# Padding the small SBUF tiles so that every large tile starts at the same byte modulo 128, in a two-layer hybrid decoder trunk

## The chip, the cores and the metric

The kernel runs on one core of a Trainium2 chip. Its engines are named as the profile names them: PE is TensorE (matrix products), PEld its weight loads, DVE is VectorE, ACT is ScalarE, POOL is GpSimd, and SP is SyncE, which issues most of the DMA transfers. The metric is the device time of one execution in microseconds (us), taken as the median of several runs. Of one execution there is a profile with the start and length of every instruction.

SBUF is the memory on the core that the engines read their operands from: 128 partitions, each a row of bytes. A tile occupies the same byte range in all partitions, so a tile has one start address. In this text "the place of a tile" is that start address modulo 128 bytes.

## What is computed

A stream of 1024 positions by 1024 channels in float32 goes through two layers, each followed by a gated MLP, with an RMS norm ahead of each part and a residual add behind it.

```python
def reference(x, ...):
    h = x
    for layer in range(DEPTH):            # DEPTH = 2
        if layer % 2 == 0:
            h = h + even_mixer(rmsnorm(h, mix0_norm), ...)
        else:
            h = h + odd_mixer(rmsnorm(h, mix1_norm), ...)
        h = h + conv_glu_ffn(rmsnorm(h, ffn_norm[layer]), ...)
    return rmsnorm(h, final_norm)

def even_mixer(x, ...):
    xa, ga, c_pre, b_post, vb = jnp.split(x @ w_in, [W, 2 * W, 2 * W + C, 2 * W + 2 * C], axis=-1)
    xa = causal_depthwise_conv(xa, lru_conv_w, lru_conv_b)
    ya = rg_lru(xa, lru_wa, lru_ba, lru_wx, lru_bx, lru_lambda) * jax.nn.gelu(ga)
    yb = b_post * causal_depthwise_conv(c_pre * vb, sconv_w, sconv_b)
    return jnp.concatenate([ya, yb], axis=-1) @ w_out

def odd_mixer(x, ...):
    z, q, k, v, f = jnp.split(x @ w_in, [Z, Z + F, Z + 2 * F, Z + 3 * F], axis=-1)
    u, g = jnp.split(jax.nn.gelu(z), 2, axis=-1)
    yc = chunked_spatial_gating(u, g, sgu_norm, sgu_w, sgu_b)   # 128-position chunks
    yd = forgetting_attention(q, k, v, f, fox_bf)               # 8 heads of 64, 128-query blocks
    return jnp.concatenate([yc, yd], axis=-1) @ w_out

def conv_glu_ffn(x, w_up, conv_w, conv_b, w_down):              # 1024 -> 2 x 2816 -> 1024
    gate, val = jnp.split(causal_depthwise_conv(x @ w_up, conv_w, conv_b), 2, axis=-1)
    return (jax.nn.silu(gate) * val) @ w_down
```

`rg_lru` makes two sigmoid gates by block-diagonal products (64x64 blocks), and runs a gated linear recurrence over the positions.

## The kernel before

Everything is kept transposed, channels on the partitions and positions along the row. Each float32 operand of a product is split into a high part (rounded to the format that PE reads in one pass) and a low part, the remainder; a product is three matmuls, high by high, high by low, low by high, each 128x128 weights by 512 positions. The normalized stream stands in `AH` (high) and `AL` (low) for the whole run. Weights come by DMA into `wst`, ACT casts the high part into `wh`, and DVE subtracts to get the low part `wl`.

The stages follow each other in program order, with each engine's instructions in the order in which the code writes them:

- **mix0** (line 1275 on): projections; for each of four channel groups the convolution `xc`, its split `xh` and `xl`, the gate products `ra` and `ix` (line 1347), and the elementwise tiles `gg`, `r`, `ig`, `w`, all from the pool `l0` that opens with the small tile `lsm` of 40 numbers.
- **out_proj0** and **blocks**: output projections into the residual tiles `hT` (`hT_o` in the traces), which `open_h` (line 308) puts at the far end of SBUF in two halves of four channel groups, each with a pool of its own. DVE adds each product to `hT` (line 557), a copy goes to DRAM, ACT squares it, and `Norm.chunk` (line 355) normalizes it into `AH` and `AL`; for four of the eight channel groups of a half POOL makes the low part.
- **ffn**: a loop over 22 groups of hidden channels with products by a seven-product scheme on blocks (line 676), results `X` and `YZ` in PSUM, DVE and ACT work on `g`, `v`, `cg`, `cv`; hidden values go to DRAM. Then eight "quads" of down-projection products (line 942) that add into `hT` (`hT_f`), and plain products (line 1152) that add the rest (line 1154). All loads of weights and hidden values are issued by SP.
- **mix1**: q, k, v and spatial-gating projections (line 1452) woven with attention. For each head, `S` is the product of `qs` with `kh` and `kl` (lines 1583 and 1584), DVE combines it with the decay row `cb` (line 1597), ACT exponentiates, PE transposes the result and multiplies it by `vv` (line 1617). The tiles of heads 3 and 7 (`qs`, `kh`, `kl`, `vv`) and `cb` of odd heads come from the pool `keep`, those of all other heads from the pool `rest`, together with the spatial-gating tiles `gain`, `wth`, `wtl`, `gsm`, `gvh`, `gvl`. The weave is a fixed list of numbers of steps and knows nothing of addresses.

Where a tile lies follows from the sizes of the tiles allocated ahead of it. The pool `const` comes first: `eps`, `junk`, `ident`, `ones`, `AH`, `AL`, the parameter columns `par_a` (96 numbers a partition), and four tiles `par_c` of the MLPs' convolution taps (88 numbers each, made in `load_rows`, line 269). Behind them come the weight buffers, the temporaries, and the stage's own pools. `hT` is allocated from the other end.

Of the kernel before, what the change touches and what calls it, by code (L numbers as in the profile page):

```python
# [8 lines left out]
F32 = mybir.dt.float32  # L9
# [7 lines left out]
P = 128  # L17
T = 1024
H = 512
D = 1024  # L20
DC = 8
NH = 8
HD = 64
DFF = 2816
NF = DFF // P
# [43 lines left out]
def weave(main, fill, pace, done=0, stop=None):  # L69


    for pos in main:
        want = pace(pos)
        while done < want and fill is not None:
            if next(fill, "end") == "end":
                fill = None
            done += 1
        if stop is not None and pos >= stop:
            break
    if fill is not None:  # L80
        run(fill)
# [75 lines left out]
def trunk(ctx: ExitStack, tc: tile.TileContext, x, mix0_norm, mix0_w_in, lru_conv_w, lru_conv_b,  # L157
# [4 lines left out]
    pe, act, dve, pool = nc.tensor, nc.scalar, nc.vector, nc.gpsimd  # L162
# [63 lines left out]
    cp = ctx.enter_context(tc.tile_pool(name="const", bufs=1))  # L226
# [8 lines left out]
    def t2(name):  # L235
        return tmp.tile([P, H], F32, tag="t2", bufs=4, name=name)
# [19 lines left out]
    def psml(name):  # L256
        return sml.tile([P, H], F32, tag="sml", name=name)
# [11 lines left out]
    def load_rows(name, groups):  # L269

        n = sum(r for _, r in groups)
        raw = t2(f"raw_{name}")[:, :P]
        at, offs = 0, []
        for ap, r in groups:
            nc.sync.dma_start(raw[at:at + r, :], ap)
            offs.append(at)
            at += r
        t = cp.tile([P, n], F32, name=f"par_{name}")
        return t, offs, raw, n

    def turn_rows(t, offs, raw, n):
        ps = psml("pt")
        pe.transpose(ps[:, :n], raw[:n, :], ident[:n, :n])
        dve.tensor_copy(t, ps[:, :n])
        return t

    def r1(ap):
# [20 lines left out]
    def open_h(name):  # L308
        st["pool"], tiles = [], []
        for i in (1, 0):  # L310
            cm = tc.tile_pool(name=f"h{i}_{name}", bufs=1, side="right")
            st["pool"].append(cm)
            tiles.insert(0, cm.__enter__().tile([P, 4, T], F32, name=f"hT{i}_{name}"))
        st["hT"] = Halves(tiles)

    def close_h():
# [102 lines left out]
    class Start:  # L419
# [68 lines left out]
        def second(self, beside):  # L488


            steps = {"q": self.squares, "r": self.root, "s": self.scale, "h": self.high,
                     "l": self.low}

            def do(ops, *behind):
                for op in ops.split():
                    with ExitStack() as after:
                        for ins in behind:
                            after.enter_context(tc.issue_after(ins.ins))
                        steps[op[0]](int(op[1]))

            behind = last["act"], last["dve"]
            do("q4 r4 q5 r5 s4 h4 l4 q6 r6 s5 h5 l5 q7 r7 s6 s7", *behind)
            do("h6 l6 h7 l7", beside(*behind))
            turn_rows(*par_rows)
            sp_cm.__exit__(None, None, None)

    norm = [Start()]
    for tt in range(4):
# [3 lines left out]
        if tt == 0:  # L512
            nc.sync.dma_start(g0, mix0_norm.partition_broadcast(P))
    W._dma()
    par_rows = load_rows("a", [
        (r1(mix0_norm), 8), (lru_conv_w[0].rearrange("k (c p) -> (k c) p", p=P), 16),
        (r1(lru_conv_b), 4), (r1(lru_ba), 4), (r1(lru_bx), 4), (r1(lru_lambda), 4),
# [12 lines left out]
    class Out:  # L530


        def __init__(self, ly):
            self.ly = ly
            open_h(f"o{ly}")
            self.hT = st["hT"]
            if ly:
                for s in HALF:
                    for c in range(DC):
                        nc.sync.dma_start(self.hT[:, c, s], hdr[:, c, s])  # L540
            g = gcols[order[order.index(f"mix{ly}") + 1]]
            self.norms = [Norm(h, g, f"no{ly}", put=True) for h in range(2)]
# [49 lines left out]
    def load_cw(ly):  # L592

        w = [ffn_conv_w[ly, k].rearrange("(c p) -> c p", p=P) for k in range(3)]
        b = ffn_conv_b[ly].rearrange("(c p) -> c p", p=P)
        rows = (load_rows(f"c{ly}0", [(w[0], 44), (w[1], 44)]),
                load_rows(f"c{ly}1", [(w[2], 44), (b, 44)]))

        def turn():
            cw[ly] = [turn_rows(*r) for r in rows]  # L600

        return turn
# [6 lines left out]
    def ffn(ly, norms):  # L609
# [469 lines left out]
        for cm in reversed(w2_cm):  # L1079
            cm.__exit__(None, None, None)  # L1080
        fd_cm.__exit__(None, None, None)
        open_h(f"f{ly}")
        hT = st["hT"]

# [190 lines left out]
    def mix0(norms):  # L1275
# [19 lines left out]
        Y = ypl.tile([P, DC, T], F32, name="Y0")  # L1295
        lp = tc.tile_pool(name="l0", bufs=1)
        pl = lp.__enter__()
        small = pl.tile([P, 40], F32, name="lsm")


        lam = par[:, o_lam:o_lam + 4]
# [114 lines left out]
    def mix1(norms):  # L1416
# [6 lines left out]
        keep, rest = keep_cm.__enter__(), rest_cm.__enter__()  # L1423
        lo, hi = slice(0, HD), slice(HD, P)

# [37 lines left out]

        fraw = rest.tile([P, DC, NH], F32, name="fraw")
        pool.dma_start(fraw, mix1_w_in[0, :, 2560:2568].rearrange("(k p) m -> p k m", p=P))
# [5 lines left out]
        dve.tensor_tensor(sel, ident[0:16, 0:8], ident[0:16, 8:16], op=ALU.add)  # L1471
        cdr = dram.tile([NH, T], F32, name="cdr")
        ydr = dram.tile([P, DC, T], F32, name="ydr")
# [30 lines left out]
        def load_c(h_):  # L1504
            cbs[h_] = (keep if h_ % 2 else rest).tile([P, T], F32, tag="cb", name=f"cb{h_}")
            nc.sync.dma_start(cbs[h_], cdr[h_:h_ + 1, :].partition_broadcast(P))

        def qkv(pr, first=False):
# [3 lines left out]
            def stack(tag, h_, shape):  # L1512
                if (tag, h_) not in stk:
                    p_, n_ = (keep, 1) if h_ % 4 == 3 else (rest, 3 if tag == "qs" else 2)
                    stk[tag, h_] = p_.tile(shape, F32R, tag=tag, bufs=n_, name=f"{tag}{h_}")
                return stk[tag, h_]

            def tail_q(ps, s, hh):
                for h_, r, nr in sides:
                    q = stack("qs", h_, [P, T])  # L1520
                    act.activation(q[r, s], ps[r], AF.Copy, scale=-(HD ** -0.5))
                    dve.scalar_tensor_tensor(q[nr, s], ps[r], -(HD ** -0.5),
                                             q[r, s].bitcast(F32), op0=ALU.mult, op1=ALU.subtract)
# [45 lines left out]
        def attn(h_):  # L1569
            qs, kh = stk["qs", h_], stk["kh", h_]  # L1570
            r0 = HD * (h_ % 2)
            rows = slice(r0, r0 + HD)
            kl, cb = stk["kl", h_], cbs[h_]
# [32 lines left out]
            def pv(g):  # L1606
# [38 lines left out]
                act.copy(yt[lo], acc[0][hi, :256])  # L1645
                if h_ == NH - 1:
                    at = rows, 7, slice(256 * g, 256 * g + 256)
# [9 lines left out]
        def chain(heads):  # L1657


            prev = None  # L1660
            for h_ in heads:
                soft, pv = attn(h_)
                n = 0
                for step in steps(soft, pv, prev, h_):
                    n += 1
                    yield h_ + min(n / 22, 0.999)
                prev = pv
            for _ in prev(3):
                n += 1
                yield h_ + min(n / 22, 0.999)  # L1670

        def steps(soft, pv, prev, h_):
# [3 lines left out]
            soft(1)  # L1676
            if h_ + 1 < NH:
                load_c(h_ + 1)
# [8 lines left out]
                yield from pv(g)  # L1687


        mhalf = rest.tile([P, 8], F32, name="mhalf")  # L1690
        pool.memset(mhalf, -0.5)

        def sgu(c):
# [22 lines left out]
            def norm_g(gz, s, hh):  # L1716
# [7 lines left out]
                v, r, q = sm[:, 0], sm[:, 1], sm[:, 2]  # L1724
                dve.tensor_reduce(v, sq.rearrange("p (n d) -> p n d", d=HD), axis=AX.X, op=ALU.add)
                dve.tensor_scalar(v, v, 1.0 / HD, EPS, op0=ALU.mult, op1=ALU.add)
# [58 lines left out]
        for _ in range(LEAD):  # L1785
            next(filler)
        heads = chain(range(NH))
        weave(heads, filler,
# [52 lines left out]
        for oc in range(DC):  # L1841
            ps = o_.block(1, oc)
# [5 lines left out]
    for s_ in order[:-1]:  # L1848
        if s_ == "mix0":
            norm = mix0(norm)  # L1850
        elif s_ == "mix1":
            norm = mix1(norm)
        else:
            norm = ffn(int(s_[-1]), norm)
# [35 lines left out]
```

## Time and profile before

| | |
|---|---|
| three runs | 2132.11, 2132.75 and 2134.26 us, median 2132.75 |
| the profiled execution | 2131.98 us, of which the profile's span is 2130.3 us |
| PE busy | 2093.4 us, 98% of the span |
| DVE busy | 1599.0 us, 75% |
| ACT busy | 1068.4 us, 50% |
| POOL busy | 75.4 us, 4% |
| DMA queues | 249.98 MB, the main one 36.5% of 16 engines |

The span runs from the first to the last instruction of the profiled execution; the 1.7 us beside it are start and end of the launch. Busy times of engines overlap, so they don't add up to the span. A group of instructions in the profile has its line, engine, operation, output and inputs, the number of instructions, their busy time in all, and the mean length of one in ns; behind it stands the idle time ahead of the group and what ended it. A busy PE is modelled: matmuls are pipelined, so a matmul of 512 columns is shown with some 390 ns although the next one starts earlier.

### The profile page before, as it was taken

To read this page: it belongs to the slowest core of one execution; us is meant where nothing else is said; L and a number is where in the kernel's file an instruction comes from. 1 tells how busy PE (TensorE), PEld (TensorE's weight loads), DVE (VectorE), ACT (ScalarE), POOL (GpSimd) and SP (SyncE) were. 2 spreads that over 40 slices of the span, in tenths; PEclk is the share of its full clock that TensorE was granted. 3 is DMA by queue.
4 is the path that set the end of the run, shared out by engine and by line. 5 is a ranking of instruction groups with operands and counts; after the bars stand their busy time and mean duration, and the time that the engine had idled before them with its cause. 6 is when DMAs were issued, how large, how long until landed. Compare 5 with 4: busy or idle time off the path is not lost. (4 is left out here: it accounts for less than half of the span.)

```text
span 2130.3 us, 25849 instructions
## 1 busy us (share of the span) xinstructions
PE 2093.4 (98%) x9673; PEld 1719.2 (81%) x9673; DVE 1599.0 (75%) x2290; ACT 1068.4 (50%) x1493; POOL 75.4 (4%) x121
## 2 busy tenths in 40 slices
PE   8999999999999999999999999999999999999998
PEld 7888888788888888888778888788788888878887
DVE  6655647998888777875566766868998888777875
ACT  5333534654555555333556575744655455555323
POOL 0000001000000000000111111101000000000000
PEclk9999999999999999999999999999999999999999
DMA  4111342333323267752221212442333233267732
GB/s 150 56 50 41 108 154 94 95 113 109 104 96 107 80 206 253 242 173 74 75 58 54 75 56 59 156 153 89 104 104 119 94 116 97 80 228 248 240 104 80
DMA packets 269318, 249.98 MB, mean 117 GB/s; under 512 B 10224, under 2 KB 222000, under 8 KB 269192
## 3 DMA queue, kind: packets, MB, share of 16 engines
q1 hardware_dynamic: 268856, 247.83, 36.5%
q8 instruction: 76, 1.25, 0.2%
q0 software_dynamic: 192, 0.30, 0.1%
q14 instruction: 50, 0.41, 0.1%
q10 hardware_dynamic: 144, 0.20, 0.0%
HBM read 181.93 MB, written 64.26 MB: 116 GB/s over the span
## 5 line engine op out<-in xcount | busy, mean ns | idle before, releaser
L129 ACT CAST wh<-wst 128x1024 fp32r<-128x1024 f32 (+1 forms) x87 | 86.3, 992 | 223.4 <-PE op L376 45.2
L129 DVE TENSOR_TENSOR wl<-wst,wh 128x1024 fp32r<-128x1024 f32 (+1 forms) x87 | 100.0, 1150 | 96.6 <-ACT wh L129 96.5
L676 PE MATMUL X<-TH,wh 128*128 128x512 f32 x384 | 150.0, 391 | 1.8 <-ACT u L1034 1.4
L676 PE MATMUL X<-TH,wl 128*128 128x512 f32 x384 | 149.7, 390 | 0.7 <-DVE wl L370 0.7
L676 PE MATMUL X<-TL,wh 128*128 128x512 f32 x384 | 149.4, 389 | 0.0
L369 ACT CAST wh<-wst 128x1024 fp32r<-128x1024 f32 x96 | 100.3, 1051 | 74.6 <-PE YZ L676 49.5
L370 DVE TENSOR_TENSOR wl<-wst,wh 128x1024 fp32r<-128x1024 f32 x96 | 116.5, 1218 | 11.9 <-ACT wh L369 11.9
L698 DVE SCALAR_TENSOR_TENSOR cg<-g,par_c,cg 128x1023 f32<-128x1023 f32 x88 | 112.8, 1281 | 7.3 <-ACT cg L692 6.1
L698 DVE SCALAR_TENSOR_TENSOR cv<-v,par_c,cv 128x1023 f32<-128x1023 f32 (+1 forms) x88 | 112.4, 1277 | 0.0
L676 PE MATMUL YZ<-AH,wh 128*128 128x512 f32 x240 | 93.5, 389 | 0.0
L676 PE MATMUL YZ<-AL,wh 128*128 128x512 f32 x240 | 93.4, 389 | 0.0
L676 PE MATMUL YZ<-AH,wl 128*128 128x512 f32 x240 | 93.4, 389 | 0.0
L1034 ACT COPY u<-X 128x512 f32<-128x512 f32 x40 | 23.6, 589 | 137.3 <-PE X L676 137.3
L676 PEld LDWEIGHTS X<-TH,wh 128*128 128x128 f32 x384 | 72.1, 188 | 18.6 <-ACT u L1034 2.6
L676 PEld LDWEIGHTS X<-TH,wl 128*128 128x128 f32 x384 | 72.1, 188 | 16.6 <-DVE wl L370 1.6
L676 PEld LDWEIGHTS X<-TL,wh 128*128 128x128 f32 x384 | 72.1, 188 | 14.8
L376 PE MATMUL op<-AH,wh 128*128 128x512 f32 x192 | 76.3, 398 | 0.6 <-ACT hT_o L551 0.6
L376 PE MATMUL op<-AH,wl 128*128 128x512 f32 x192 | 74.9, 390 | 0.0
L376 PE MATMUL op<-AL,wh 128*128 128x512 f32 x192 | 74.8, 389 | 0.0
L1056 DVE TENSOR_TENSOR v<-p,u 128x512 f32<-128x512 f32 x40 | 27.6, 691 | 57.6 <-ACT u L1049 57.6
L692 ACT ACTIVATE cg<-g,par_c 128x1024 f32<-128x1024 f32 x44 | 54.8, 1246 | 29.4 <-DVE g L1058 24.7
L1600 ACT ACTIVATE P<-P,sm 128x128 f32<-128x128 f32 (+3 forms) x64 | 49.7, 777 | 30.0 <-DVE sm L1597 29.6
(779 smaller groups left out, 6301.9 us busy)
## 6 DMA issues: line engine op xcount, KB each, us to landing
wst<-in_ffn_up_dram SPq DMA_DIRECT2D x88, 512.0 KB
br<-hids SPq DMA_DIRECT2D x56, 512.0 KB
wst<-in_mix_w_in_dram SPq DMA_DIRECT2D x40, 512.0 KB
wst<-in_mix_w_out_dram SPq DMA_DIRECT2D x32, 512.0 KB
hids<-cv SPq DMA_DIRECT2D x32, 512.0 KB
hdr<-hT_o SPq DMA_DIRECT2D x32, 256.0 KB
hids<-t SPq DMA_DIRECT2D x32, 256.0 KB
hd<-hdr SPq DMA_DIRECT2D x16, 512.0 KB
```

The costliest lines, as they stand in the source:

```text
L129: did = self.nc.scalar.copy(wh[:, :k, :m], w[:, :k, :m]), self.eng.tensor_tensor(wl[:, :k, :m], w[:, :k, :m], wh[:, :k, :m].bitcast(F32), ...
L369: return (act.copy(h, src), (eng or dve).tensor_tensor(l, src, h.bitcast(F32), op=ALU.subtract))
L370: (eng or dve).tensor_tensor(l, src, h.bitcast(F32), op=ALU.subtract))
L376: last_mm = pe.matmul(ps, a[:, k], b[:, k, s], start=(k == 0 and i == 0), stop=(k == DC - 1 and i == 2))
L676: last = pe.matmul(ps, a[:, k0 + k], b[:, k], start=(first and k == 0 and i == 0), stop=(k == 3 and i == 2), skip_group_check=True)
L692: act.activation(self.cg, self.g, AF.Identity, scale=taps[2](f), bias=bias(f))
L698: dve.scalar_tensor_tensor(dst[:, dl:], src[:, :T - dl], taps[j](c), dst[:, dl:], op0=ALU.mult, op1=ALU.add)
L1034: u2_ = act.copy(u2, X)
L1056: dve.tensor_tensor(v[:, HALF[1]], p5, u3, op=ALU.add)
L1600: act.activation(Pt[:, :n], Pt[:, :n], AF.Exp, bias=low, scale=-1.0, accum_out=sm[:, 6:7])
```

## The change

It pads. The columns of the parameter tiles are rounded up to a multiple of 32 numbers (128 bytes), so that the four `par_c` tiles take 384 bytes each instead of 352 (`par_a` already has 384). `lsm` grows from 160 to 256 bytes, and `mhalf`, the first of mix1's `rest` tiles behind the small ones, from 32 to 64. The tile of the upper half of `hT`, at the far end of SBUF, gets 32 bytes more, of which nothing is used. All uses take the same part of a tile as before. The instructions, their order, their shapes, and their waits on semaphores are the same ones; what differs is the addresses in them. No address in PSUM or DRAM changes.

Places of the tiles, worked out from the sizes:

| tiles | place before | place after | moved by, bytes |
|---|---|---|---|
| `AH`, `AL`, `ident`, `ones`, `par_a` | 64 | 64 | 0 |
| four `par_c` | 64, 32, 0, 96 | 64 | 0, +32, +64, +96 |
| weights `wst`, `wh`, `wl`; all temporaries; `TH`, `TL`, `Y`, `cg`, `cv`; attention's `keep` pool | 64 | 64 | +128 |
| mix0's gate tiles `xc`, `xh`, `xl`, `gg`, `r`, `ig`, `w` and gate weights | 96 | 64 | +224 |
| attention's `rest` pool: `qs`, `kh`, `kl`, `vv` of heads 0, 1, 2, 4, 5, 6, `cb` of even heads, spatial gating's tiles | 32 | 64 | +160 |
| `hT`, all four allocations, both halves | 96 | 64 | -32 |

Modulo 64, the third row's tiles stay at 0, and the last three rows' tiles go from 32 to 0. Modulo 256, tiles of the third row change between 192 and 64.

```diff
+LINE = 32
...
-        t = cp.tile([P, n], F32, name=f"par_{name}")
+        t = cp.tile([P, -(-n // LINE) * LINE], F32, name=f"par_{name}")
         return t, offs, raw, n
 
     def turn_rows(t, offs, raw, n):
         ps = psml("pt")
         pe.transpose(ps[:, :n], raw[:n, :], ident[:n, :n])
-        dve.tensor_copy(t, ps[:, :n])
+        dve.tensor_copy(t[:, :n], ps[:, :n])
...
         for i in (1, 0):
             cm = tc.tile_pool(name=f"h{i}_{name}", bufs=1, side="right")
             st["pool"].append(cm)
-            tiles.insert(0, cm.__enter__().tile([P, 4, T], F32, name=f"hT{i}_{name}"))
+            t = cm.__enter__().tile([P, 4 * T + i * LINE // 4], F32, name=f"hT{i}_{name}")
+            tiles.insert(0, t[:, :4 * T].rearrange("p (c t) -> p c t", c=4))
...
-        small = pl.tile([P, 40], F32, name="lsm")
+        small = pl.tile([P, 2 * LINE], F32, name="lsm")
...
-        mhalf = rest.tile([P, 8], F32, name="mhalf")
+        mhalf = rest.tile([P, LINE // 2], F32, name="mhalf")[:, :8]
```

## Prediction

> **What bounds the kernel.** First the page: the busy times, the granted clock and the chain that ended last.
>
> ```profile
> span 2130.3 us, 25849 instructions
> ...
> PE 2093.4 (98%) x9673; PEld 1719.2 (81%) x9673; DVE 1599.0 (75%) x2290; ACT 1068.4 (50%) x1493; POOL 75.4 (4%) x121
> ...
> PEclk9999999999999999999999999999999999999999
> ...
> PE 31%; DVE 3%; ACT 1%; DMA 1%; issue 1%; POOL 0%; DVEq 0%; ACTq 0%; SPq 0%
> ```
>
> PE is busy for 2093.4 of 2130.3 us at full clock, so 36.9 us of the span are idle PE; everything that the other engines and the DMA could give back by being faster lies in those 36.9 us. The chain confirms it as far as the view goes (its shares add up to 37% of the span, the last 795 us): PE holds 31%, DVE 3%, ACT and DMA 1% each. Next the view of waits, for PE alone, whose first two rows are these:
>
> ```profile
> PE xp L455 <- DVE xn L446: 4.7, 3, 1.8
> PE S L1583 <- DVE sm L1597: 3.5, 6, 1.0
> ```
>
> No single wait is worth 5 us; the idle time is crumbs, most of them at the start, in attention and at the end. The other 98% are matmuls, so I look at the price of one, in the groups by shape. The MLP loop has most of them:
>
> ```profile
> L676 PE MATMUL X<-TH,wh 128*128 128x512 f32 x384 | 150.0, 391 | 1.8 <-ACT u L1034 1.4 <-ACT u L995 0.4
> ...
> L676 PE MATMUL YZ<-AL,wh 128*128 128x512 f32 x240 | 93.4, 389 | 0.0
> ```
>
> All operands here (`TH`, `AL`, `wh`) lie at place 64 before and after. What the change can touch is the length of single instructions whose operands move, and how instructions that run side by side disturb each other.
>
> **The change, part by part.** It removes, adds and reorders nothing, on any engine or queue, and no wait changes; no sum over instructions taken away or put in arises. The terms are differences of length, place 32 or 96 against place 64. The trace of before holds both places side by side, so most of them can be read.
>
> *DVE and ACT on `hT`* (96 now, 64 after), from the groups by shape, each with a group of the same shape that works on tiles at 64:
>
> ```profile
> L370 DVE TENSOR_TENSOR AL<-br,AH 128x1024 fp32r<-128x1024 f32 x32 | 38.6, 1219 | 5.2 <-ACT AH L369 5.2
> ...
> L1058 DVE TENSOR_TENSOR g<-YZ,u 128x512 f32<-128x512 f32 x40 | 27.3, 684 | 4.4 <-PE YZ L676 4.2
> ...
> L369 ACT CAST dh<-s 128x512 fp32r<-128x512 f32 x42 | 26.2, 623 | 23.7 <-PE YZ L676 19.4 <-DVE s L648 3.6
> ...
> L1154 DVE TENSOR_TENSOR hT_f<-dp,hT_f 128x512 f32<-128x512 f32 x32 | 22.1, 689 | 19.8 <-PE dp L1152 19.7
> ...
> L369 ACT CAST AH<-hT_o 128x512 fp32r<-128x512 f32 x32 | 19.9, 622 | 27.6 <-DVE hT_o L355 27.0
> L1103 DVE TENSOR_TENSOR hT_f<-hT_f,hd 128x1024 f32<-128x1024 f32 x16 | 19.5, 1217 | 0.0
> ```
>
> A sum of 1024 columns in SBUF takes 1217 ns on `hT_f` and 1219 on `br`; an addition of 512 columns out of PSUM takes 689 ns on `hT_f` and 684 on `g`; a cast of 512 columns 622 ns from `hT_o` and 623 from `s`. The largest difference is 5 in 689, 0.7%, the two others have the opposite sign. If all idle PE time were waits on such instructions, 0.7% of 36.9 us would be 0.3 us. The term lies between -0.3 and +0.3 us; I take 0, by the nearest rows.
>
> *mix0's gate products* have both operands at 96. The view of the tile `xh` gives shortest, median and longest:
>
> ```profile
> L1347 PE MATMUL ra<-xh,gwha x8: 387/390/397, 59.1 to 231.7; 128*128 128x512 f32 x8
> ...
> L1347 PE MATMUL ra<-xh,gwla x8: 389/397/398, 59.9 to 232.2; 128*128 128x512 f32 x8
> ...
> L1347 PE MATMUL ix<-xh,gwhx x8: 389/389/389, 60.8 to 233.1; 128*128 128x512 f32 x8
> ```
>
> Medians are 390, 397 and 389 ns beside 389 to 391 in the loop. The mean of the three, 392, is 3 ns over 389; that is what the place could cost at most.
>
> *Attention* offers the cleanest pair: head 2 has `qs`, `kh`, `kl`, `vv` and `cb` at place 32, head 3 has all of them at 64 already. The groups by shape in the stretch of head 2, 1136.5 to 1176.5 us (line, operation, count, busy time, mean):
>
> ```profile
> L1597 DVE CUSTOM_DVE_ANT_0 P<-cb,S 128x512 f32<-128x512 f32 x4 | 2.7, 682 | 0.1
> ...
> L1584 PE MATMUL S<-kl,qs 128*128 128x512 f32 x6 | 2.4, 394 | 0.0
> L1583 PE MATMUL S<-kh,qs 128*128 128x512 f32 x6 | 2.4, 393 | 0.0
> ```
>
> and of head 3, 1181.5 to 1218 us:
>
> ```profile
> L1597 DVE CUSTOM_DVE_ANT_0 P<-cb,S 128x512 f32<-128x512 f32 x4 | 2.7, 683 | 1.8 <-PE S L1584 1.8
> ...
> L1583 PE MATMUL S<-kh,qs 128*128 128x512 f32 x6 | 2.4, 405 | 0.0
> L1584 PE MATMUL S<-kl,qs 128*128 128x512 f32 x6 | 2.3, 391 | 0.0
> ```
>
> At the old place the products take 393 and 394 ns, at the new one 405 and 391, and the DVE pass 682 and 683. The new place wins nothing; with six products in a row, one that came late makes the 12 ns. So PE's term: matmuls that read a moved tile are 192 of `S`, 320 with `vv`, 48 gate products, 48 of spatial gating and 64 transposes of `hT`, 672 counted in the kernel's loops. With 3 ns each as the upper end it is -2.0 us; with head 3's excess, (405 - 393 + 391 - 394) / 2 = 4.5 ns, it is +3.0 us. Between these I take 0: the two ends come from single late instructions, and the gate rows lie at 389 and 390 for most.
>
> *POOL's part of the norm* is the one group where a moved tile looks slow. The view of the tile `AL` for POOL:
>
> ```profile
> L370 POOL TENSOR_TENSOR AL<-hT_o,AH x8: 1301/1844/2271, 322.0 to 1448.1; 128x512 fp32r<-128x512 f32 x8
> L370 POOL TENSOR_TENSOR AL<-y_nf,AH x4: 1283/1288/1292, 983.7 to 1004.0; 128x512 fp32r<-128x512 f32 x4
> ```
>
> Reading `hT_o` takes a median of 1844 ns, reading `y_nf` at place 64 takes 1288. By place the gain would be 8 x 0.55 = 4.4 us of POOL; but one of the eight took 1301 at the same place, so the rest is waiting for something else that runs. Nothing on PE's path feels either: this runs beside PE's products of the other half (POOL is 4% busy, and PE's waits name no such row). If that cover were gone, one instruction, 0.6 us, would show at each norm's end. I take 0.
>
> *Transfers.* Those that fill or empty `hT` and the `rest` tiles change their place, and nearly all tiles change modulo 256 (192 and 64 swap). The chain of waits has transfers at these points, us from the start, length, what:
>
> ```profile
> 1369.59 4.35 DMA yr<-ydr
> ...
> 1895.06 4.66 DMA br<-hids
> ...
> 1905.61 6.35 DMA x21104A<-in_ffn_down_dram
> ```
>
> The densest stretch loads `hT_o` at its old place. SP's timeline issues nine of these loads from here:
>
> ```profile
> 1370.77 4.95 SPq L540 DMA_DIRECT2D hT_o<-hdr  x9
> ```
>
> and the table by windows (PE, PEld, DVE, ACT, POOL busy, clock, DMA share, GB/s) gives for the stretch in which they land:
>
> ```profile
> 1378.00:1382.00 4.00, 4.00 (x20) 3.29 (x21) 2.93 (x9) 2.53 (x4) 0.00 (x0) 1.00 1.02 385
> ```
>
> 385 GB/s at a share of 1.02 is 377 GB/s for full engines. The quads, with loads and stores at place 64, move 204 at 0.62, which is 329 (their row stands below). So the old place doesn't hold transfers up. As an upper end, 13%, the spread of these two rates, on the chain's DMA share (1%, 21 us) would be 2.8 us to either side; I take 0, since the faster stretch is that of the old place.
>
> **The sum**: profiled execution 2131.98 us + 0 = 2131.98. The median of the three runs is 0.77 above the profiled one, so the median to expect is 2132.7 us.
>
> One thing moves by itself. The table by windows at the end of attention:
>
> ```profile
> 1358.00:1364.00 6.00, 4.18 (x25) 3.14 (x23) 5.55 (x15) 5.93 (x10) 1.04 (x2) 1.00 0.67 199
> 1364.00:1368.00 4.00, 3.96 (x18) 3.24 (x17) 3.87 (x15) 3.94 (x11) 0.42 (x1) 0.57 0.92 305
> ```
>
> For 4 us the granted clock is 0.57, after a stretch in which PE was busy for 4.18 of 6 us. That costs up to 0.43 x 4 = 1.7 us. The three runs lie 2.15 us apart, room for one dip more or less. [...]
>
> **The rivals.**
>
> *Place decides contention, and the kernel gets faster.* Single instructions may be alike, while engines that stream from different places disturb each other. In attention, where tiles at 32 and 64 mix, the matmuls on tiles at 64 are longer than in the loop:
>
> ```profile
> L1452 PE MATMUL 1u<-AH,wh 128*128 128x512 f32 x64 | 26.6, 416 | 0.0
> ...
> L1452 PE MATMUL 1u<-AH,wl 128*128 128x512 f32 x64 | 25.4, 397 | 0.0
> ...
> L1452 PE MATMUL 1u<-AL,wh 128*128 128x512 f32 x64 | 25.1, 392 | 0.0
> ```
>
> If all of that came from neighbours at place 32, it would go: (416 + 397 + 392 - 3 x 389) = 38 ns a triple, at most 5 projections x 64 triples, 12.2 us, so 2132.7 - 12.2 = 2120.5. Against it: the excess sits on the first of each triple, which follows the transposes and small products woven in; and in mix0, with neighbours at 96, gate medians are 389 to 397. Chance 6%; another 2% for a gain beyond 0.2% that no row shows.
>
> *All tiles at one place disturb each other, and the kernel gets slower.* Where `hT` is read and written beside products, its words now start where those of `AH` and `AL` do. The stages with `hT`, in the table by windows:
>
> ```profile
> 240.00:345.00 105.00, 104.26 (x490) 86.14 (x489) 73.90 (x86) 49.15 (x74) 7.69 (x4) 1.00 0.46 141
> 800.00:925.00 125.00, 124.05 (x548) 102.72 (x548) 102.82 (x120) 54.45 (x67) 0.94 (x1) 1.00 0.73 242
> 925.00:1010.00 85.00, 85.00 (x373) 69.66 (x372) 49.71 (x67) 26.03 (x37) 5.15 (x4) 1.00 0.36 109
> 1402.00:1470.00 68.00, 68.00 (x303) 55.92 (x302) 45.90 (x57) 28.27 (x38) 7.07 (x4) 1.00 0.47 149
> 1920.00:2070.00 150.00, 150.00 (x663) 124.24 (x663) 118.19 (x146) 57.32 (x73) 0.00 (x0) 1.00 0.62 204
> ```
>
> They hold 490 + 548 + 373 + 303 + 663 = 2377 matmuls. If each grew by the 3 ns by which `1u<-AL,wh` exceeds 389, that is 7.1 us, so 2139.8. It decides from 2 ns a matmul on. Against it: in the MLP loop DVE and ACT already work at the same place as PE, and the matmuls have 389 to 391. Chance 4%.
>
> *Transfers gain by the 128 bytes.* From the rows above between 0 and -2.8 us, down to 2129.9, still within 0.2%. [...] Chance 3%.
>
> **How the numbers follow.** Nothing to see: 85%, and with the transfers 88% for within 0.2% of 2132.75 (2128.5 to 2137.0, about what a measurement of this kernel tells from no change). Faster 8%, slower 4%. The range takes the terms' ends together with the clock's 1.7 us and the runs' own spread of 2.15 us, which do not all fall to one side: 2129.5 to 2136.0. It leaves out the two rivals on contention, 12% with what no row shows.
>
> **What the profile of after would show.** Right: the six groups on `hT` keep their means to 1%, heads 2 and 3 remain alike, `ra` keeps 390 and 397, the triple of `1u` stays near 416, 397, 392, the five windows keep their idle time. Contention is right if the triple falls to 389 or the stages with `hT` shorten; lockstep, if matmuls there rise over 391. Transfers: the waits for `yr` and `br` become shorter. The prediction is wrong if the median leaves 2128.5 to 2137 with the clock as before.

## The result and the profile after

The kernel became slower: median 2161.06 us (2160.38 to 2162.03, four runs) beside 2132.43 us (2131.74 to 2134.26, four runs) of the kernel before, a ratio of 1.0133 with an interval of 1.0116 to 1.0151, or 28.6 us. The prediction, 2132.7 us within 2129.5 to 2136.0, missed it.

The page of the changed kernel, its busy times, granted clock and chain:

```profile
span 2159.3 us, 25849 instructions
...
PE 2124.6 (98%) x9673; PEld 1720.3 (80%) x9673; DVE 1603.9 (74%) x2290; ACT 1066.7 (49%) x1493; POOL 74.7 (3%) x121
...
PEclk9999999999999999999999999999999999999999
...
PE 35%; ACT 1%; DVE 1%; issue 0%; DMA 0%; POOL 0%; DVEq 0%; ACTq 0%
```

The number of instructions is the same, and the clock stands at 9 (90% or more) in every slice, as before. PE is busy for 31.2 us more (2093.4 before), while its idle time is 2159.3 - 2124.6 = 34.7 us, 2.2 less than before. So no wait was added: PE's own work became longer. The groups by shape say which. Here are two of the MLP loop and the three of `1u` in attention, after:

```profile
L678 PE MATMUL X<-TH,wh 128*128 128x512 f32 x384 | 150.3, 391 | 1.8 <-ACT u L1036 1.4 <-ACT u L997 0.4
...
L678 PE MATMUL YZ<-AL,wh 128*128 128x512 f32 x240 | 94.7, 394 | 0.0
...
L1454 PE MATMUL 1u<-AH,wh 128*128 128x512 f32 x64 | 26.6, 416 | 0.0
...
L1454 PE MATMUL 1u<-AH,wl 128*128 128x512 f32 x64 | 25.5, 398 | 0.0
...
L1454 PE MATMUL 1u<-AL,wh 128*128 128x512 f32 x64 | 25.2, 393 | 0.0
```

Products with `TH` stayed at 391 ns; products with `AL` went from 389 to 394. Five nanoseconds look like nothing, but the shown length of a matmul is modelled. What counts in a row of matmuls is the time from one start to the next. The timeline of PE in the last quads shows it directly; the first and the last of 15 rows in a row, before:

```profile
1999.82 0.39 PE L942 MATMUL dq114A<-AH,wl 128*128 128x512 f32 x1
...
2003.00 0.39 PE L942 MATMUL dq114A<-AL,wh 128*128 128x512 f32 x1
```

and after:

```profile
1999.64 0.40 PE L944 MATMUL dq110A<-AH,wl 128*128 128x512 f32 x1
...
2002.91 0.40 PE L944 MATMUL dq110A<-AL,wh 128*128 128x512 f32 x1
```

Each stretch is fourteen steps of the same kind (the blocks are named `dq114A` and `dq110A`). They take 3.18 us before, 227 ns each, and 3.27 us after, 234 ns each, although nothing waits.

Then all steps of the two traces were grouped by the addresses of their operands: the start of the moving operand (`AH`, `AL`, `TH` and so on) and the start of the weights that PE loads beside it, which are those of the next matmul, both modulo 256 bytes. (In the stretch before, the load of the weights for the matmul that starts at 2000.05 us is shown from 1999.83 us on with 0.19 us, beside the matmul that starts at 1999.82.) The addresses are those that the kernels allocate; the trace doesn't hold them. Columns: kernel, start of moving operand, start of weights, number of steps (128x512 with such matmuls on both sides, groups of more than ten with these starts), median from start to start in ns.

```
before   192  192   7888   227
before   192   64     14   232
after     64   64   2191   227      (TH, TL with wh, wl)
after    192   64   5658   232      (AH, AL with wh, wl)
after     64  192    166   232
after    192  192     30   233
```

Before, nearly all pairs lay at the same byte modulo 256. After, `AH` and `AL` still lie at 192, while weights and temporaries moved by 128 bytes to 64. Of all 8452 matmuls of 128x512, whatever their neighbours, 187 stood beside weights at another byte before, and 6178 after. 5991 more steps, 5 ns each, are 30 us. The drift between the two traces, taken matmul by matmul, fits. At 80 us of the trace of before, the one of after is 2.5 us behind (a dip of its clock at 35 us has a share in that), at 1075 us 17.6 us, at 1340 us 18.05 us, at 1400 us 17.9 us, and at the last matmuls 29.1 us. So it grows all along except in attention (1075 to 1395 us), where PE also waits (8.2 us idle of 320) and where the median step of the projections was 231 ns before already and is 232 ns after.

### The profile page after: what moved, and what is told of

It is laid out like the page before. It is cut to its first block, busy times and chain, and to the rows that moved or that the text cites. A ratio compares the mean times of both kernels' runs of the same rounds, so it can differ in the third digit from the quotient of the medians.

```text
span 2159.3 us, 25849 instructions
## 1 busy us (share of the span) xinstructions
PE 2124.6 (98%) x9673; PEld 1720.3 (80%) x9673; DVE 1603.9 (74%) x2290; ACT 1066.7 (49%) x1493; POOL 74.7 (3%) x121
## 5 line engine op out<-in xcount | busy, mean ns | idle before, releaser
L678 PE MATMUL YZ<-AH,dl 128*128 128x512 f32 x160 | 63.2, 395 | 0.0
```

What stands on the lines that cost most here:

```text
L678: last = pe.matmul(ps, a[:, k0 + k], b[:, k], start=(first and k == 0 and i == 0), stop=(k == 3 and i == 2), skip_group_check=True)
```

## The experiments

Three theories stood against each other. **R**: a matmul is long where its moving operand and the weights loaded beside it start at different bytes modulo 256. **W**: weights at byte 64 modulo 256 are slow in themselves. **L**: the rival of the prediction, lockstep of tiles that all lie at one place modulo 128. Each ratio is against executions of the kernel before that were taken together with it; their medians lie between 2132.4 and 2137.1 us.

**The shift without the alignment.** 128 bytes in front of the weights, and no other part of the change:

```diff
-        t = cp.tile([P, n], F32, name=f"par_{name}")
+        t = cp.tile([P, n + 32 * (name == "a")], F32, name=f"par_{name}")
...
-        dve.tensor_copy(t, ps[:, :n])
+        dve.tensor_copy(t[:, :n], ps[:, :n])
```

> The kernel before, with par_a 128 bytes longer: weights, temporaries and all later tiles of that side move by 128 bytes, as the change moves them; hT, the gate tiles and attention's rest tiles keep their places 96, 96 and 32 relative to 128. Theory R (a matmul takes some 5 ns longer from start to start where its moving operand and the weights that PE loads beside it start at different bytes modulo 256; AH and AL stay at 192, weights go to 64): 2161 us, +28. Theory L (the change is slow because hT, gates and attention now start at the same byte modulo 128 as the rest and engines disturb each other): 2132 us. Theory W (weights at byte 64 modulo 256 are slow by themselves): 2161 us.

Measured: 1.0125 (1.011 to 1.0141), 2163.43 beside 2136.45 us. The whole loss is there, with `hT`, the gates' and attention's tiles at places of their own. L falls.

**The change, with 128 bytes more.** Everything in the changed kernel, and `par_a` longer by `LINE` numbers, so that the weights come back to byte 192:

```diff
-        t = cp.tile([P, -(-n // LINE) * LINE], F32, name=f"par_{name}")
+        t = cp.tile([P, -(-n // LINE) * LINE + LINE * (name == "a")], F32, name=f"par_{name}")
```

> The change, with par_a 128 bytes longer still: weights and temporaries have moved by 256 in all and are at 192 modulo 256 again, as AH and AL; every large tile still starts at 64 modulo 128. Theory R: 2132 us, the 28 us are gone, a few us less if the products of attention and gates, now at equal bytes modulo 256 more often, count. Theory L: 2161 us. Theory W: 2132 us.

Measured: 0.9997 (0.9987 to 1.0006). The loss is gone, with all tiles at one place modulo 128. Alignment modulo 128 itself is worth nothing here that can be told from zero, to either side (-2.8 to +1.3 us).

**`AH` and `AL` moved along.** The weights stay at byte 64, where they were slow, and `AH`, `AL` follow them there, by a longer `eps` at the front of the pool:

```diff
-    eps = cp.tile([P, 1], F32, name="eps")
+    eps = cp.tile([P, 8 + LINE], F32, name="eps")[:, :1]
...
-        t = cp.tile([P, -(-n // LINE) * LINE], F32, name=f"par_{name}")
+        t = cp.tile([P, n], F32, name=f"par_{name}")
```

> The change's addresses for the weights, the temporaries and everything behind them (64 modulo 256), but ident, ones, AH and AL are moved by 128 bytes too, to 64 modulo 256 (the tile eps is longer, the par_c tiles have their old length). Theory R: 2132 us. Theory W: 2161 us. Theory L: 2161 us.

Measured: 1.0001 (0.9992 to 1.0011). The groups by shape have the loop's products back at 389 ns, with weights at byte 64:

```profile
L678 PE MATMUL YZ<-AH,wh 128*128 128x512 f32 x240 | 93.5, 389 | 0.0
L678 PE MATMUL YZ<-AL,wh 128*128 128x512 f32 x240 | 93.4, 389 | 0.0
```

W falls: it isn't where the weights lie, but where they lie relative to the moving operand.

**PE by itself.** This run's kernel has no transfer of data and no DVE or ACT work beside these matmuls. The granted clock is 0.976 in the mean of the run's 245.0 us; the warm-up series at the start has 432 ns a matmul, while `movoo`, from 26.1 us on, and `last`, at the end, both have 389 ns, as the loop of the kernel before. Each series keeps one shape and shifts the moving operand (`mov`), the weights (`wts`) or both (`two`), by multiples of 32 bytes, or by a few numbers (`fine`):

```
...
for k, nm in enumerate(BY32):
    series("mov" + nm, lambda i: far(i, 8 * k), lambda i: wide(i, 0))
...
    series("wts" + nm, lambda i: far(i, 0), lambda i: wide(i, 8 * k))
...
    series("two" + nm, lambda i: far(i, 8 * k), lambda i: wide(i, 8 * k))
...
```

> The layers are left out; PE alone runs series of 24 matmuls 128x128 by 512 in the same number format, with nothing beside them: the moving operand shifted by 0, 32, .. 224 bytes against the weights, the weights against the moving operand, both together, and two series of 48 where each third matmul has its weights or its moving operand 128 bytes off. Theory R: start to start 227 ns at a shift of 0 and with both shifted alike, 232 ns at 128, and the other shifts tell the period. Theory W: only the weights' place counts, the shifted moving operand stays at 227. If the 5 ns need another engine beside PE (theory L), all series stay at 227.

The groups by shape, the last number before the second bar being the mean length in ns. `oo` is a shift of 0, `fd` of 64, `ab` of 128 and `al` of 192 bytes:

```profile
L48 PE MATMUL moval<-mv,wt 128*128 128x512 f32 x24 | 5.8, 394 | 0.0
...
L48 PE MATMUL wtsab<-mv,wt 128*128 128x512 f32 x24 | 5.8, 395 | 0.0
...
L48 PE MATMUL movab<-mv,wt 128*128 128x512 f32 x24 | 5.8, 395 | 0.0
...
L48 PE MATMUL movfd<-mv,wt 128*128 128x512 f32 x24 | 5.7, 392 | 0.0
...
L48 PE MATMUL twoab<-mv,wt 128*128 128x512 f32 x24 | 5.6, 390 | 0.0
...
L48 PE MATMUL movoo<-mv,wt 128*128 128x512 f32 x24 | 5.6, 389 | 0.0
```

Either operand 128 bytes off makes 395 of 389, whichever it is; both off together make 390. From start to start the means are 226.7 (`movoo`), 233.5 (`movab`, `wtsab`), 227.8 (`twoab`, at 224 to 236 for its first seven steps and at 226 to 227 from there on) and 229.3 ns (`movfd`). The eight `two` series cover all starts by 32 bytes, and from the seventh step on each of them has 227: no byte is slow in itself. So the price belongs to the pair, and is there with no other engine busy (395 beside 389 ns). Of the two series with every third matmul off, the one with the moving operand off has one step in three long (234 beside 226 to 227 ns); the one with the weights off settles, after some thirteen irregular steps, at two in three (232 to 235 beside 226 to 227). The operands step by 256 bytes (moving) and 512 bytes (weights) within a series, and `movoo` is still fast: only the byte modulo 256 counts.

In the series that shift every matmul a step takes 2 to 10 ns more (229 to 237 beside 227) as soon as the moving operand and the weights start at different bytes modulo 256; where they start at the same one, these runs can't show whether the load of the next weights costs anything.

**The dose: temporaries alone.** 128 bytes in front of the temporaries, so that `TH`, `TL` and what lies behind them (`dh`, `dl` too) part from the weights:

```diff
     tmp = ctx.enter_context(tc.tile_pool(name="tmp", bufs=1))
+    tmp.tile([P, 32], F32, tag="off", name="off_t")
```

> The kernel before with 128 bytes in front of its temporaries alone: TH, TL and what lies behind them move to byte 64 modulo 256, the weights and AH, AL stay at 192. Of PE's 128x512 steps some 2900 more than before now read a moving operand that lies elsewhere, modulo 256, than the weights that PE loads beside it: the products with TH and TL, and the FFN's products with dh and dl, which lie behind them. Theory R (the cost is that of a pair, 4.7 ns a step as in the run of the changed kernel, 28.6 us over some 6000 such steps): 2900 x 4.7 ns, +13.6 us, between +11 and +16; X<-TH rows at 394 to 396 ns instead of 389 to 391, YZ<-AH,wh still 389. Rival D (any move of large tiles by 128 bytes away from AH's place costs the same loss): +28 us. Rival W (only weights that lie at 64 modulo 256 cost): no change.

Measured: 1.0068 (1.0053 to 1.0083), 14.5 us by the ratio. The groups have changed sides, `TH` and `dh` long, `AH` with `wh` short:

```profile
L677 PE MATMUL X<-TH,wh 128*128 128x512 f32 x384 | 151.8, 395 | 1.8 <-ACT u L1035 1.4 <-ACT u L996 0.4
...
L677 PE MATMUL YZ<-AH,wh 128*128 128x512 f32 x240 | 93.6, 390 | 0.0
...
L677 PE MATMUL YZ<-AH,dl 128*128 128x512 f32 x160 | 63.1, 395 | 0.0
```

**The dose: weights alone.** The same pad in front of the pool of weights, and one more in front of the temporaries, which brings these back:

```diff
     wpool = ctx.enter_context(tc.tile_pool(name="wp", bufs=1))
+    wpool.tile([P, 32], F32, tag="off", name="off_w")
     tmp = ctx.enter_context(tc.tile_pool(name="tmp", bufs=1))
+    tmp.tile([P, 32], F32, tag="off", name="off_t")
```

> The kernel before with 128 bytes in front of the pool of weights and 128 more behind it: wst, wh and wl move to byte 64 modulo 256, everything else keeps its byte (AH, AL, TH, TL, dh, dl at 192). Some 6490 steps more than before lie on a pair that differs: all products with wh or wl, the ones with TH now too. Theory R: 6490 x 4.7 ns, +30.5 us, between +27 and +39 (the TH steps are in stages where PE never waits, so they may count in full); X<-TH,wh at 395 instead of 391, and YZ<-AH,dh unchanged at 390 to 394. Rival D (what counts is how many tiles moved, and here fewer move than in the change): less than the change's 28 us, some +10 to +20 us.

Measured: 1.0132 (1.0117 to 1.0147), 28.2 us. By the number of tiles moved, some 10 to 20 us had been expected; R's 30.5 lies in the interval (25.0 to 31.4 us). In the groups all products with `wh` are long, the ones with `dl` are not:

```profile
L678 PE MATMUL X<-TH,wh 128*128 128x512 f32 x384 | 152.2, 396 | 1.8 <-ACT u L1036 1.4 <-ACT u L997 0.4
...
L678 PE MATMUL YZ<-AH,wh 128*128 128x512 f32 x240 | 94.8, 395 | 0.0
...
L678 PE MATMUL YZ<-AH,dl 128*128 128x512 f32 x160 | 62.6, 391 | 0.0
```

**The dose: `wl` alone.** One product in three has its weights moved:

```diff
+        pair = []
+        for t in ("wh", "wl"):
+            pair.append(self.pool.tile([P, DC, P], F32R, tag=t, bufs=3, name=f"{t}{n}"))
+            if n == 0:
+                self.pool.tile([P, 32], F32, tag="off" + t, name="off" + t)
+        return pair
```

> The kernel before with 128 bytes between wh and wl and 128 behind wl: only wl moves, to byte 64 modulo 256. The products run wh with AH, wh with AL, wl with AH, and round again. If only the weights that PE loads during a matmul, those of the next one, count against its moving operand (R, next), a step in three is long: 2200 more than before x 4.7 ns, +10.4 us, and YZ<-AL,wh alone (the one ahead of wl) is at 395. If a matmul's own weights count as well (R, both; the series of matmuls alone, in which every third weights lay 128 bytes off, showed two steps of three long), 4300 x 4.7 ns, +20 us, and YZ<-AH,wl is at 395 too. Rival: if only own weights count, +10 us, with YZ<-AH,wl alone at 395.

Measured: 1.0086 (1.0069 to 1.0102), 18.4 us. The groups:

```profile
L680 PE MATMUL YZ<-AH,wl 128*128 128x512 f32 x240 | 95.3, 397 | 0.0
L680 PE MATMUL YZ<-AL,wh 128*128 128x512 f32 x240 | 95.0, 396 | 0.0
L680 PE MATMUL YZ<-AH,wh 128*128 128x512 f32 x240 | 93.5, 390 | 0.0
```

Two products of three are long, not one: `AL` with `wh`, during which `wl` is loaded, and the one behind it, whose own weights are `wl`. From start to start the medians are 233 and 234 ns, and 227 for `AH` with `wh`. So the weights of the next matmul are not the whole rule, and 20 us was the nearest of the three expectations. Whether the second long step comes from its own weights or only follows from the first, this run can't tell.

**The distance.** `par_a` longer by 48 numbers (192 bytes) and by 16 (64 bytes), otherwise as in the shift alone. The moving operand `AH` then lies 64 bytes behind the weights (at the higher byte), or 64 ahead of them:

```diff
+        t = cp.tile([P, n + 48 * (name == "a")], F32, name=f"par_{name}")
```

> The kernel before with par_a 192 bytes longer instead of the 128 of the run with the shift alone: weights and temporaries lie at byte 128 modulo 256, and AH, AL at 192, 64 bytes further than the weights. In the series of matmuls alone a moving operand 64 bytes behind the weights took 229 ns a step (227 with none, 233 with 128). Theory R with that table: 6000 steps x about 2 ns, +12 us, between +7 and +16; YZ<-AH,wh at 391 to 392. Rival (any difference at all costs the same): +28 us, YZ<-AH,wh at 395. Rival (only a difference of 128 bytes costs): no change.

> The kernel before with par_a 64 bytes longer: weights and temporaries at byte 0 modulo 256, AH and AL at 192, so that the moving operand lies 64 bytes ahead of the weights (192 behind). By the series of matmuls alone (233 ns a step at 192 behind, 229 at 64 behind, 227 at none): as long as with 128 bytes, 6000 steps x 4.7 ns, +28 us, between +24 and +33, YZ<-AH,wh at 395. Rival (the price goes by the distance, 64 bytes either way): as the run with 192 bytes, +13 us.

Measured: with 192 bytes 1.0063 (1.0048 to 1.0078), 13.5 us; with 64 bytes 1.0126 (1.0109 to 1.0143), 26.9 us. The distance has a sign, as in the series alone (392 ns for 64 bytes behind, 394 and 396 for 64 ahead). The three products of `YZ` with 192 bytes have 394, 392 and 389 ns: 392 in the mean, as the series had it, but not one like the other. One thing in the run with 192 bytes was not expected, in its groups by shape:

```profile
L676 PE MATMUL X<-TH,wh 128*128 128x512 f32 x384 | 152.4, 397 | 1.8 <-ACT u L1034 1.4 <-ACT u L995 0.4
L676 PE MATMUL X<-TH,wl 128*128 128x512 f32 x384 | 151.2, 394 | 0.3
L676 PE MATMUL X<-TL,wh 128*128 128x512 f32 x384 | 149.6, 390 | 0.0
```

Here `TH`, `wh` and `wl` all lie at byte 128 modulo 256, and two of three are long all the same. They run between stretches of `AH`, whose pairs do differ. That byte 128 is slow in itself is no way out: in `movoo` both operands start there, at 227 ns a step. Of these products, 118 stretches of the MLP loop have twelve steps each. The medians over the stretches, by place in the stretch, from start to start in ns:

```
before                227 227 227 227 227 227 227 227 227 227 227 227
with 192 bytes        234 231 233 236 224 231 236 228 233 231 227 227
with 64 bytes         226 236 228 233 231 226 227 227 226 227 227 226
the change            232 233 231 227 227 227 227 227 227 227 227 227
```

The pairs in these stretches are alike in all four kernels. The stretch begins out of step, by what the `AH` products ahead of it left, and falls back to 227 ns after ten, five or three steps.

**Patterns.** Series of 48 matmuls in which single operands are 128 bytes off:

```
one = lambda i: i % 6 == 5
...
series("wone", no, one)                          # one of six weights off
series("mone", one, no)                          # one of six moving operands off
series("both", one, one)                         # both of the same matmul
...
series("mwnext", lambda i: i % 6 == 4, one)      # a moving operand, and the weights of the next matmul
...
series("blocks", no, lambda i: i % 24 >= 12)     # twelve on, twelve off
...
```

> All layers are left out; series of 48 matmuls alone, both tiles at the same byte modulo 256 and single operands 128 bytes off. Theory R, next (the weights loaded during a matmul, those of the next one, against its moving operand): weights off once in six (wone): the step ahead of them is at 232 to 234 ns, the five others at 227; moving operand off once in six (mone): its own step alone; both off in one matmul: only the step ahead of it; a moving operand off and the weights of the next one off as well (mwnext): none long. Theory R, both (a matmul's own weights count too): wone two steps of six, both: one or two of six, mwnext two of six. Rival H (a disturbed step leaves the next ones out of step until they fall back): in wone two or more steps behind the first are long, with sizes that run out, and in blocks the first steps of the twelve undisturbed ones are long too. With fewer columns the matmul is shorter than the load of 128 weights at some point: at 128 columns no difference between on and off is expected (the earlier steps of 109 to 111 ns at 128 columns had both kinds); at 384 and 256 some 3 to 6 ns if the price belongs to the load, and less in proportion if it belongs to the columns streamed.

The groups by shape; `on` and `off` are series with fewer columns (`three` 384, `two` 256):

```profile
L43 PE MATMUL blocks<-mv,wt 128*128 128x512 f32 x48 | 11.3, 393 | 0.0
...
L43 PE MATMUL wone<-mv,wt 128*128 128x512 f32 x48 | 11.1, 392 | 0.0
...
L43 PE MATMUL mone<-mv,wt 128*128 128x512 f32 x48 | 11.1, 390 | 0.0
L43 PE MATMUL threeoff<-mv,wt 128*128 128x384 f32 x48 | 8.6, 338 | 0.0
L43 PE MATMUL threeon<-mv,wt 128*128 128x384 f32 x48 | 8.5, 334 | 0.0
L43 PE MATMUL twoon<-mv,wt 128*128 128x256 f32 x48 | 5.9, 283 | 0.0
L43 PE MATMUL twooff<-mv,wt 128*128 128x256 f32 x48 | 5.9, 281 | 0.0
```

and the steps from start to start in ns, in order, of `wone` from its seventh matmul and of `blocks` from its twelfth (those of the weights off are 12 to 23):

```
wone     227 226 227 227 232 234 | 227 227 226 227 232 235
blocks   233 | 240 233 231 231 229 230 232 241 233 230 232 233 | 236 224 231 236 228 233 231 226 227 227 226 233
```

In `wone` two steps of six are long: the one during which the shifted weights are loaded, and the next one. In `mone` it is one, its own. In `blocks` the rule of the pair alone fails: for seven steps after the weights are back, the steps still vary between 224 and 236, and only then they return to 227. A disturbed row leaves the following matmuls out of step for a while, as the `TH` stretches do in the kernels: their ten steps with 192 bytes hold the same run of numbers (236 224 231 236 228 233 231) as the seven behind the weights in `blocks`.

Two more series went against the rule of the pair in both its forms. In `mwnext`, R by the next weights expected no long step and R with a matmul's own weights two of six; in `both`, one or two of six were expected. Measured, the row never comes back to a steady 227: the steps lie between 224 and 236 ns, with medians of 230 (`mwnext`) and 231 (`both`), those of equal pairs among them. With disturbances six matmuls apart, one is not over when the next one comes, while in `wone` and `mone` it is. So the pair tells where a disturbance starts and, in long rows of one kind, what it costs in the mean; the length of a single step it doesn't tell. What the state is that carries over stays open. With 256 columns (119 and 120 ns a step) and 128 columns (112 and 112) nothing is lost, with 384 columns 3 ns (176 beside 173; 4 ns in the lengths shown). A load of 128x128 weights is shown with 188 ns in the MLP loop of before, longer than the steps of all three.

**The change without its rounding of the parameter tiles.** The other three paddings stay:

```diff
-        t = cp.tile([P, -(-n // LINE) * LINE], F32, name=f"par_{name}")
+        t = cp.tile([P, n], F32, name=f"par_{name}")
```

> The change with one of its parts undone: the columns of the parameter tiles aren't rounded up, so that the 128 bytes ahead of the weights are gone; the other paddings (hT, lsm, mhalf) stay. Weights and temporaries are back at byte 192 modulo 256 beside AH and AL; of 8452 steps 56 have a pair that differs, before had 187. Theory R: no loss, 0 us against the kernel before, between -2 and +2. Any theory by which the places of hT, the gates' or attention's tiles cost: part or all of the 28 us stays.

Measured: 0.9996 (0.9987 to 1.0005). One line of the change makes its whole loss: the four `par_c` tiles grow by 32 bytes each, 128 bytes in all, and lie between `AL` and the weights.

**All tiles at one byte modulo 256.** The change, `par_a` longer by 128 bytes, and attention's two pools shifted as well:

```diff
-                sm = keep.tile([P, 8], F32, tag="sm", bufs=4, name=f"sm{h_}{j}")
+                sm = keep.tile([P, LINE // 2], F32, tag="sm", bufs=4, name=f"sm{h_}{j}")[:, :8]
...
-        mhalf = rest.tile([P, LINE // 2], F32, name="mhalf")[:, :8]
+        mhalf = rest.tile([P, LINE // 2 + LINE], F32, name="mhalf")[:, :8]
```

> The change with 128 bytes more in par_a, in the four sm tiles together and in mhalf, so that all large tiles, attention's th, tl, qs, kh, kl and vv among them, start at byte 192 modulo 256: the aim of the change, with 256 in the place of 128. 26 steps of 8452 keep a pair that differs (before 187). Theory R: attention's projections, in which the median step was 229 ns before because the products woven in had differing pairs, fall to 227; 868 x 2 ns and 160 x 5 ns make 2.5 us at most, in a stage where PE also waits; between -2.5 and 0 us, hardly to be told from no change. Rival (the woven steps are long for another reason): 0.

Measured: 0.9999 (0.999 to 1.0008). Nothing to gain: the median step of attention's projections, over all 1056 of them, is 231 ns here and before, so the woven products there are long for another reason than the pairs, which stays open. The kernel before had all but 187 of its 8452 pairs at one byte already; no version of these beat it.

## Why the prediction was wrong

The step that failed stands in the part on what bounds the kernel: "All operands here (`TH`, `AL`, `wh`) lie at place 64 before and after. What the change can touch is the length of single instructions whose operands move". It judged places modulo 128, the change's own measure, and so took the loop's matmuls, the bulk of PE's time, as untouched. Modulo 256 `AL` stayed at 192 and `wh` went to 64. The part on transfers says that "nearly all tiles change modulo 256 (192 and 64 swap)" and draws no line from it to PE.

- *PE's term* followed from that. It counted 672 matmuls that read a tile moved modulo 128 and gave them -2.0 to +3.0 us. (By its own measure the count is 544: heads 3 and 7, whose tiles keep their place, are counted in.) The steps concerned were 5991, at 5 ns. That the size per matmul comes near the ends considered (3 and 4.5 ns) is chance, since those were read from other matmuls for another reason; the count was off by a factor of nine, and the wrong matmuls were counted.
- *The rows that priced place* could not show the cost. The gate products have moving operand and weights both at byte 96 modulo 256, `S` of head 2 has both at 160, and `S` of head 3 both at 64. Each compares one equal pair with another.
- *The row that could have warned* was in the trace of before. 38 of its 128x512 steps had weights 128 bytes off the moving operand, with a median of 232 ns, beside 227 for the 8265 at the same byte. Only start-to-start times by pair show it; in the groups by shape they vanish among the rest.
- *DVE and ACT on `hT`, gates, attention*: these terms were 0, and stayed 0. The sums on `hT_f` take 690 and 1218 ns (689 and 1217 before), the casts from `hT_o` 620 (622), `ra` 390 and 393 (390 and 397); in head 2 `S` keeps 393 and 394, in head 3 it has 406 and 394 (405 and 391). The triple of `1u` stays near 416, 398, 393, as the prediction said it would if place did not decide contention there.
- *POOL's part of the norm*, held for waiting and not for place, keeps long ones with `hT_o` at its new place. The view of `AL` for POOL, after:

```profile
L372 POOL TENSOR_TENSOR AL<-hT_o,AH x8: 1298/1720/2280, 329.8 to 1466.8; 128x512 fp32r<-128x512 f32 x8
L372 POOL TENSOR_TENSOR AL<-y_nf,AH x4: 1286/1288/1296, 1000.0 to 1020.9; 128x512 fp32r<-128x512 f32 x4
```

- *Transfers* have no row of their own in these runs. With `AH` and `AL` moved along, weights and temporaries lie at 64 modulo 256 as in the change, without PE's loss, and the time is that of before (1.0001, interval -1.7 to +2.3 us). So the rival "Transfers gain by the 128 bytes" gave nothing of its end of -2.8 us; whether a transfer's length depends on its place modulo 256 was not shown.
- *The rival "All tiles at one place disturb each other"* had the sign, and not the mechanism. It put the loss into the stages with `hT` and priced it at 7.1 us; the shift alone, with `hT` where it was, lost all of it. The evidence cited against it, matmuls of 389 to 391 ns in the loop beside DVE and ACT at the same place, speaks to engines that disturb each other, and none did: the series of PE alone pay the same price.
- *The clock* is as the prediction had it. Besides the last microseconds, both traces have one stretch of 4 us with a granted clock of 0.57, before from 1364 to 1368 us and after from 35 to 39 us: the dip moved, and by the prediction's estimate it is worth at most 1.7 us in either. The clock also differs without any change of addresses: over 19 executions of the kernel before, its mean lies between 0.995 and 0.999. What brings a dip on was not shown.

## What to carry to other kernels

Where PE runs 512-column matmuls one behind the other, each with weights of its own, in the rounded number format used here (the series had no other), the moving operand and the weights should start at the same byte modulo 256 (227 ns a step here, beside 229 to 237); look at the distance between the two, not at the alignment of each. A small tile that grows between them can cost more than a per cent, as here (1.0133), and the profile shows it as no wait at all. In a row of matmuls compare times from start to start, grouped by the addresses of both operands, since the lengths shown are modelled.

## What the runs showed of the hardware

- The price by distance, from the series of PE alone, moving operand minus weights in bytes modulo 256, mean length shown in ns: 0: 389; 4: 398; 8 and 32: 395; 16: 394; 48, 64, 80 and 112: 392; 96: 396; 128: 395; 160: 396; 192: 394; 224: 395; 240: 396. Equal is a narrow case; the smallest distance costs the most, and several between 48 and 112 cost half.
- It is a matter of long rows: at a distance of 128 bytes, 128x512 costs 7 ns of 227 in a steady row, 128x384 3 ns of 173, 128x256 and 128x128 nothing.
- It outlasts its cause by up to ten matmuls: a stretch of twelve at the same byte is out of step for three to ten steps behind a row whose pairs differ.
- A product of two tiles in the rounded format, 128x128 by 512, is one matmul in the traces, with 227 ns from start to start. The norm's product of `ones` and the sum of squares (line 344), of the same shape in plain float32, is two matmuls there, shown with 590 ns or more and, in four of six such products, 428 or 429 ns apart.
